# Differential attention: the probability tiles transposed by DMA from SBUF halves instead of by TensorE

## The chip, the cores and the metric

The kernel runs on one core of one Trainium2 chip. The metric is the device time of one execution in microseconds (us). Times of the kernel before are the median of three runs; one further execution was recorded by the hardware profiler, and all rows below come from it.

## The reference, cut to what matters

The program is a two-layer block of a diffusion transformer on 512 latent and 256 context tokens of width 1024. Layer 1 ends in a mixture of experts. Before that it has two kinds of attention side by side: a windowed attention, and the differential attention that this change concerns:

```python
def diff_attend(q, kvs, lam):
    ss = [einsum('bhiqd,bhikd->bhiqk', q, k) * scale for k, _ in kvs]
    ps = joint_softmax(ss)                       # over latent and context keys together
    for p, (_, v) in zip(ps, kvs):
        a = p[:, :, 0] - lam * p[:, :, 1]        # two softmaxes, subtracted
        out = out + einsum('bhqk,bhkd->bhqd', a, v)
```

There are 4 heads, each with two softmaxes over 768 keys, and 512 queries. Everything is float32 to the outside; the kernel splits each operand of a matmul into two float16 halves, `hi` and `lo = x - hi`.

## The kernel before, in words

The program is written for a framework that takes the instructions in the order of the Python code, gives each tile a buffer out of a pool, and then orders each engine's queue itself. Each engine runs its queue in order.

`diff` (line 1393) handles 4 blocks of 128 queries with 8 units each: unit m is one softmax of one head, so two units, a pair, make one head. 16 pairs follow each other, counted here from 0 to 15. For a pair:

- `scores` (L1422): eight matmuls (L770) write both units' scores `dS`, 128 x 768 float32 each, into PSUM. There are two such buffers, so the next pair's first matmul waits for this pair's exponentials.
- `probs` (L1432): VectorE takes the row maximum (L1435, `dnm`), ScalarE the exponential (L1438, `dP`) with the row's sum. The even unit's tile is `P0`. For the odd unit VectorE makes a factor out of both sums (L1443, L1444, `dden`), and GpSimd multiplies P by it (L1446) and adds P0 (L1447). P0's pool has 4 buffers.
- `transp` (L1450): calls `p_transp` (L1351). TensorE transposes P in six 128 x 128 float32 chunks into two PSUM tiles `PT` of three chunks (L1360); for each of them ScalarE writes `Phi`, the float16 half (L1361), and VectorE subtracts to get `Plo` (L1362), both out of PSUM. Phi and Plo have 2 buffers each.
- `pv` (L1457): twelve matmuls (L1467, L1468) multiply the six chunks of Phi and Plo with the values into `dO`.

`attention` (L772) emits, at step i, scores of unit i, transp of unit i - DLAG[1], and pv of unit i - DLAG[2]. After the last head of a query block a chain of small VectorE operations (L1481 to L1490, `rs_of` at L315, with names dr, dss, rs_v, rs_r, rs_t, don) normalizes it, and L1383 to L1390 put it into `yT`.

`layer1` (L1516) runs the first units beside the last projection (`psdv`, the values, L347 to L349, with L637 and L638 after each token tile), then the rest of the pairs, and then interleaves the end of `diff` with the first half of the output projection `od_out(0)` (tile `odps`, L342) by the weights DIFF_W and OUT_W. Beside it GpSimd gathers the residual `h` from DRAM (L1560) and SyncE loads weights (`wst`, L246) that ScalarE and VectorE split into halves (`whi` L269, `wlo` L274). SyncE's queue is in order as well: a load waits there until its buffer's last split is done.

Of the kernel before, what the change touches and what calls it, by code (L numbers as in the profile page):

```python
# [12 lines left out]
F16 = mybir.dt.float16  # L13
BF = mybir.dt.bfloat16
I32 = mybir.dt.int32
AF = mybir.ActivationFunctionType
OP = mybir.AluOpType
# [25 lines left out]
PB2 = 6  # L43
NLAG = (0, 3, 4)
SLAG = (0, 2, 3)
DLAG = (0, 6, 8)

GEMM_W, SWA_W, DIFF_W, OUT_W = 42.0, 50.0, 40.0, 24.0
NDIF = 4

NSTEP1 = (0, 2, 3, 3)
# [254 lines left out]
class K:  # L306
# [1086 lines left out]
    def diff(self, T, yT, ap, p2, pp, tpb):  # L1393
        nc = self.nc
        Qd, Kd, Vd = T['dq'], T['dk'], T['dv']
        units = [dict(q=n, m=m) for n in range(4) for m in range(8)]
        den, O, osum, P0 = {}, {}, {}, {}
        pend = []

        def flush(d=3):  # L1400
            for p in pend:
                p[0] += 1
            while pend and pend[0][0] > d:
                z = pend.pop(0)
                z[1]()
                self.ndiff = z[2] + 1

        def products(u):
            n, m = u['q'], u['m']
            if m == 0:  # L1410
                den[n] = ap.tile([128, 8], F32, name=f"dden{n}", tag="den", bufs=2)
            u['S'] = ps = pp.tile([128, 1024], F32, name=f"dS{n}_{m}", tag="S", bufs=2)
            qs = slice(n * 128, n * 128 + 128)
            b = 64 * (m % 2)
            full, half = [], []
            for bank, (k0, kn) in enumerate(CHUNKS):
                o = ps[:, k0:k0 + kn]
                full.append((o, Qd[:, m, qs], Kd[:, m, k0:k0 + kn], bank))
                half.append((o, Qd[b:b + 64, m, qs], Kd[b:b + 64, 8 + m // 2, k0:k0 + kn], bank))
            return full, half  # L1420

        def scores(u):  # L1422
            if u['m'] % 2:
                return 0.0
            i = 8 * u['q'] + u['m']
            pair = units[i:i + 2]
            self.paired(*[products(z) for z in pair])
            for z in pair:
                probs(z)
            return 1.2  # L1430

        def probs(u):  # L1432
            n, m, ps = u['q'], u['m'], u.pop('S')
            nm = ap.tile([128, 1], F32, name="dnm", tag="dnm", bufs=4)
            nc.vector.tensor_reduce(out=nm, in_=ps[:, 0:NT], axis=AX.X, op=OP.max, negate=True)  # L1435
            P = (p2 if m % 2 else ap).tile([128, 768], F32, name="dP", tag="P", bufs=PB2 if m % 2 else PB)
            dn = den[n][:, m:m + 1]
            nc.scalar.activation(P, ps[:, 0:NT], AF.Exp, bias=nm, accum_out=dn)  # L1438
            if m % 2 == 0:
                P0[n] = P  # L1440
            else:

                nc.vector.reciprocal(dn, dn)  # L1443
                nc.vector.scalar_tensor_tensor(out=dn, in0=dn, scalar=self.nlam, in1=den[n][:, m - 1:m], op0=OP.mult,  # L1444
                                               op1=OP.mult)
                nc.gpsimd.tensor_scalar(P, P, dn, 1.0, op0=OP.mult, op1=OP.mult)  # L1446
                nc.gpsimd.tensor_tensor(out=P, in0=P, in1=P0[n], op=OP.add)  # L1447
                u['P'] = P

        def transp(u):  # L1450
            if u['m'] % 2 == 0:
                return 0.0
            flush()
            u['PT'] = self.p_transp(u.pop('P'), 6, ap, pp, tpb)
            return 0.65

        def pv(u):  # L1457
            n, m = u['q'], u['m']
            if m % 2 == 0:
                return 0.0  # L1460
            hd = m // 2
            hi, lo = u.pop('PT')
            if hd % 2 == 0:
                O[n] = pp.tile([128, 2, 2, 128], F32, name=f"dO{n}_{hd}", tag="G", bufs=2)
            o = O[n][:, hd % 2]
            for i in range(6):
                nc.tensor.matmul(o, hi[:, i, :], Vd[:, i, hd], start=i == 0, stop=False)  # L1467
                nc.tensor.matmul(o[:, 0, :], lo[:, i, :], Vd[:, i, hd, 0], start=False, stop=i == 5)  # L1468
            if hd == 0:
                osum[n] = ap.tile([128, 4, 128], F32, name=f"osum{n}", tag="osum", bufs=1)  # L1470
            if hd % 2 == 1:
                nc.vector.tensor_reduce(out=osum[n][:, hd - 1:hd + 1], in_=O[n].rearrange("p h s d -> p h d s"),
                                        axis=AX.X, op=OP.add)
            if hd == 3:
                os_ = osum[n]
                sq = ap.tile([128, 4, 128], F32, name="dsq", tag="dsq", bufs=1)
                ss = ap.tile([128, 4], F32, name="dss", tag="dss", bufs=2)
                for i in range(4):
                    nc.scalar.activation(sq[:, i], os_[:, i], AF.Square, accum_out=ss[:, i:i + 1])
                r0 = ap.tile([128, 4], F32, name="dr0", tag="dr0", bufs=2)  # L1480
                nc.vector.reciprocal(r0, den[n][:, 0:8:2])  # L1481
                r2 = ap.tile([128, 4], F32, name="dr2", tag="dr2", bufs=2)
                nc.vector.tensor_tensor(out=r2, in0=r0, in1=r0, op=OP.mult)
                nc.vector.tensor_tensor(out=ss, in0=ss, in1=r2, op=OP.mult)
                rs = self.rs_of(ap, ss, 4, 128, "sub")
                nc.vector.tensor_tensor(out=rs, in0=rs, in1=r0, op=OP.mult)
                for i in range(4):
                    nc.scalar.activation(os_[:, i], os_[:, i], AF.Copy, scale=rs[:, i:i + 1])
                on = ap.tile([128, 512], F32, name="don", tag="dsq", bufs=1)
                nc.vector.tensor_tensor(out=on.rearrange("p (h d) -> p h d", h=4), in0=os_,  # L1490
                                        in1=self.gsub.unsqueeze(1).broadcast_to([128, 4, 128]), op=OP.mult)
                self.o_out(on, 512, yT, 4, n, ap, pp, pend, tpb)
                pend[-1].append(n)
            return 1.0

        yield from self.attention(units, [scores, transp, pv], DLAG)
        flush(0)

# [570 lines left out]
```

## Time and profile before

| what | us |
|---|---|
| median of 3 runs | 1780.31 |
| lowest and highest of them | 1778.89, 1789.47 |
| profiled execution, its own time | 1788.69 |
| its span, first to last instruction | 1786.8 |
| mean granted TensorE clock in it | 0.977 of full |

The page of the profile has the busy time of each engine, then the span in 40 slices of 44.7 us, in which a digit is the busy tenths of that slice. The differential attention lies at 1113.9 to 1224.5 us, in the slices 25 to 28 (the first slice is 1). Idle time in a row is that just before the instruction, with what released it.

### The profile page before, as it was taken

To read this page: it belongs to the slowest core of one execution; us is meant where nothing else is said; L and a number is where in the kernel's file an instruction comes from. 1 tells how busy PE (TensorE), PEld (TensorE's weight loads), DVE (VectorE), ACT (ScalarE), POOL (GpSimd) and SP (SyncE) were. 2 spreads that over 40 slices of the span, in tenths; PEclk is the share of its full clock that TensorE was granted. 3 is DMA by queue.
4 is the path that set the end of the run, shared out by engine and by line. 5 is a ranking of instruction groups with operands and counts; after the bars stand their busy time and mean duration, and the time that the engine had idled before them with its cause. 6 is when DMAs were issued, how large, how long until landed. Compare 5 with 4: busy or idle time off the path is not lost. (4 is left out here: it accounts for less than half of the span.)

```text
span 1786.8 us, 36195 instructions
## 1 busy us (share of the span) xinstructions
PE 1668.7 (93%) x15124; PEld 1170.3 (65%) x15124; DVE 1251.0 (70%) x2463; ACT 883.1 (49%) x1420; POOL 156.1 (9%) x102
## 2 busy tenths in 40 slices
PE   3999999999999999999999999989789999999997
PEld 1444666555566665555555466447579988989997
DVE  6784899877665444333147999696898588788884
ACT  6564555262222222111254667564666577677773
POOL 1100000000000000000000000451210113101201
PEclk9999999999999999999999999999799999999999
DMA  8413342534333442233312201101569788899893
GB/s 322 160 51 100 104 166 95 212 117 143 142 129 131 142 142 96 73 112 112 115 61 79 95 1 48 70 3 54 189 204 337 240 312 334 303 330 336 313 337 109
DMA packets 51801, 286.82 MB, mean 161 GB/s; under 512 B 5824, under 2 KB 10944, under 8 KB 27568
## 3 DMA queue, kind: packets, MB, share of 16 engines
q1 hardware_dynamic: 47328, 271.74, 41.8%
q0 software_dynamic: 3296, 10.95, 2.7%
q8 instruction: 120, 1.97, 0.4%
q10 hardware_dynamic: 1008, 1.77, 0.3%
q14 instruction: 49, 0.40, 0.1%
HBM read 272.57 MB, written 11.08 MB: 159 GB/s over the span
## 5 line engine op out<-in xcount | busy, mean ns | idle before, releaser
L342 PEld LDWEIGHTS <-whi 128*128 128x128 f16 x5184 | 469.7, 99 | 185.3 <-issue 10.8
L342 PE MATMUL f<-yT,whi 128*128 128x512 f16 (+1 forms) x1408 | 325.5, 326 | 1.5 <-ACT af L438 1.5
L342 PEld LDWEIGHTS <-wlo 128*128 128x128 f16 x2592 | 255.6, 99 | 90.4 <-issue 2.2
L274 DVE SCALAR_TENSOR_TENSOR wlo<-wst,whi 128x512 f16<-128x512 f32 (+2 forms) x154 | 236.8, 1549 | 68.1 <-ACT whi L269 67.6
L269 ACT ACTIVATE whi<-wst 128x2048 f16<-128x2048 f32 (+2 forms) x152 | 199.4, 1331 | 111.1 <-PE f L342 72.8
L342 PE MATMUL f<-yT,wlo 128*128 128x512 f16 (+1 forms) x704 | 229.1, 326 | 0.0
L375 DVE SCALAR_TENSOR_TENSOR adjk<-wst,srow 128x1024 bf16<-128x1024 f32 x96 | 117.3, 1221 | 98.4 <-DMA wst<-in_w_adr_dram 97.2
L342 PE MATMUL f<-gT,whi 128*128 128x512 f16 (+1 forms) x704 | 164.4, 326 | 0.0
L342 PE MATMUL mps<-xT,whi 128*128 128x176 f16 (+6 forms) x1472 | 149.0, 229 | 3.8 <-DVE mgf L1848 3.7
L342 PE MATMUL mps<-xT,wlo 128*128 128x176 f16 (+6 forms) x736 | 143.0, 229 | 0.0
L342 PE MATMUL f<-gT,wlo 128*128 128x512 f16 (+1 forms) x352 | 114.7, 326 | 0.0
L342 PEld LDWEIGHTS <-aT 128*128 128x128 f16 x1584 | 106.8, 99 | 5.3 <-issue 4.5
L467 DVE TENSOR_TENSOR h<-h,ytp 128x256 f32<-128x256 f32 (+1 forms) x48 | 24.3, 507 | 109.2 <-PE ytp L465 108.9
L2019 POOL DMA_INDIRECT out_dram<-yr,sidx x14 | 54.4, 3885 | 358.3 <-DVE yr L1884 215.3
L342 PE MATMUL cvps<-aT,whi 128*128 128x512 f16 (+1 forms) x384 | 82.6, 328 | 2.8 <-ACT Kl L632 2.3
L342 PEld LDWEIGHTS <-whix 128*128 128x128 f16 x992 | 81.4, 98 | 2.9 <-issue 2.5
L1082 ACT CAST gT<-g 128x512 f16<-128x512 f32 (+1 forms) x23 | 14.0, 608 | 131.0 <-DVE g L1079 131.0
L274 DVE SCALAR_TENSOR_TENSOR wlo<-wstx,whi 128x2048 f16<-128x2048 f32 (+2 forms) x42 | 68.7, 1651 | 14.0 <-ACT whi L269 11.4
L342 PE MATMUL mps<-xT,aT 128*128 128x176 f16 (+6 forms) x1056 | 74.4, 231 | 2.3 <-DVE mgf L1848 2.3
L342 PE MATMUL mps<-mgT,whi 128*128 128x176 f16 (+6 forms) x704 | 73.0, 227 | 0.9 <-ACT mgT L1853 0.9
L342 PE MATMUL mps<-mgT,wlo 128*128 128x176 f16 (+6 forms) x352 | 68.1, 227 | 0.0
L269 ACT ACTIVATE whi<-wstx 128x2048 f16<-128x2048 f32 (+2 forms) x42 | 57.7, 1401 | 17.6 <-PE mps L342 16.3
(398 smaller groups left out, 3490.1 us busy)
## 6 DMA issues: line engine op xcount, KB each, us to landing
wst<-in_w_m_dram SPq DMA_DIRECT2D x38, 1024.0 KB, 6.2
wstx<-in_w_m_dram SPq DMA_DIRECT2D x33, 1024.0 KB, 6.2
wst<-in_w_adr_dram SPq DMA_DIRECT2D x32, 1024.0 KB, 4.9
wst<-in_w_f_dram SPq DMA_DIRECT2D x22, 1024.0 KB, 4.8
wst<-in_w_m_dram SPq DMA_DIRECT2D x27, 704.0 KB, 6.0
wstx<-in_w_m_dram SPq DMA_DIRECT2D x25, 704.0 KB, 6.1
aT<-in_w_m_dram SPq DMA_DIRECT2D x17, 1024.0 KB, 6.2
wst<-in_w_ada_dram SPq DMA_DIRECT2D x12, 1024.0 KB, 4.9
```

Of the source, the lines that this page charges most:

```text
L269: nc.scalar.activation(h, x, AF.Copy, scale=self.scale)
L274: nc.vector.scalar_tensor_tensor(out=l, in0=x, scalar=SW, in1=h, op0=OP.mult, op1=OP.subtract)
L342: mm(ps[:, s0:s0 + sn], w[:, k, :], a[:, kk, s0:s0 + sn], start=first and p == 0, stop=last and p == 2)
L375: nc.vector.scalar_tensor_tensor(out=jk, in0=st[:, j * D:(j + 1) * D], scalar=1.0, in1=self.srow[:, t, :], op0=OP.mult, op1=OP.mult, accum ...
L467: nc.vector.tensor_tensor(out=hs, in0=hs, in1=tp[:, 0:w].rearrange("p (t c) -> p t c", t=nt), op=OP.add)
L1082: nc.any.tensor_copy(gh, g[:, 0:sn])
L2019: self.nc.gpsimd.indirect_dma_start(out=to, out_offset=bass.IndirectOffsetOnAxis(ap=self.sidx[0:sn, e, s:s + 1], axis=0), in_=yr[0:sn, s, ...
```

## The change

`transp` no longer calls `p_transp`. ScalarE copies the finished P, in SBUF, to float16 in one instruction over all 768 columns (after: L1457), VectorE subtracts that from P in one instruction over SBUF operands (after: L1458), and both halves go into the 3072 bytes a row of the pair's P0 tile, which is free once GpSimd has added it. SyncE then issues two transposing DMAs, SBUF to SBUF, 128 x 768 float16 each (192 KB), into Phi and Plo (after: L1462). P0's buffer is free again only when both have landed. The distance DLAG[1] goes from 6 units to 4, and DIFF_W from 40 to 30, as transp's own weight goes from 0.65 to 0. `swa` still uses `p_transp`.

```diff
-DLAG = (0, 6, 8)
-GEMM_W, SWA_W, DIFF_W, OUT_W = 42.0, 50.0, 40.0, 24.0
+DLAG = (0, 4, 8)
+GEMM_W, SWA_W, DIFF_W, OUT_W = 42.0, 50.0, 30.0, 24.0
...
-                u['P'] = P
+                u['P'], u['P0'] = P, P0[n]
...
             flush()
-            u['PT'] = self.p_transp(u.pop('P'), 6, ap, pp, tpb)
-            return 0.65
+            P = u.pop('P')
+            z = u.pop('P0').bitcast(F16).rearrange("p (z c) -> p z c", z=2)
+            nc.scalar.activation(z[:, 0], P, AF.Copy)
+            nc.vector.tensor_tensor(out=z[:, 1], in0=P, in1=z[:, 0], op=OP.subtract)
+            u['PT'] = []
+            for i, nm in enumerate(("Phi", "Plo")):
+                t = ap.tile([128, 6, 128], F16, name=nm, tag=nm, bufs=2)
+                nc.sync.dma_start_transpose(out=t, in_=z[:, i])
+                u['PT'].append(t)
+            return 0.0
```

VectorE's queue in the third query block, at the row maxima of the pair with units 4 and 5 and the small chain of the first block; before:

```order
L1435 TENSOR_REDUCE dnm<-dS_4_12248 128x1
L331 TENSOR_TENSOR rs_t<-rs_r 128x4
L1444 SCALAR_TENSOR_TENSOR dden_12148<-dden_12148,nlam 128x1
L332 SCALAR_TENSOR_TENSOR rs_t<-rs_t,rs_v 128x4
L1435 TENSOR_REDUCE dnm<-dS_5_12249 128x1
L333 SCALAR_TENSOR_TENSOR rs_r<-rs_t,rs_r 128x4
L1362 TENSOR_TENSOR Plo<-PT,Phi 128x384
L1486 TENSOR_TENSOR rs_r<-rs_r,dr_12119 128x4
L1362 TENSOR_TENSOR Plo<-PT,Phi 128x384
L1435 TENSOR_REDUCE dnm<-dS_6_12297 128x1
```

The same place in the changed kernel:

```order
L1435 TENSOR_REDUCE dnm<-dS_4_12198 128x1
L331 TENSOR_TENSOR rs_t<-rs_r 128x4
L1444 SCALAR_TENSOR_TENSOR dden_12114<-dden_12114,nlam 128x1
L332 SCALAR_TENSOR_TENSOR rs_t<-rs_t,rs_v 128x4
L1435 TENSOR_REDUCE dnm<-dS_5_12199 128x1
L333 SCALAR_TENSOR_TENSOR rs_r<-rs_t,rs_r 128x4
L1458 TENSOR_TENSOR dP<-dP 128x768
L1495 TENSOR_TENSOR rs_r<-rs_r,dr_12085 128x4
L1435 TENSOR_REDUCE dnm<-dS_6_12239 128x1
```

The two subtractions from PSUM have become one from SBUF; what stands around it is as before. Four of the sixteen new subtractions stand further ahead, among the last row maxima beside the values' projection, and the one below is the fourth of them, with the split of an output weight behind it:

```order
L1458 TENSOR_TENSOR dP<-dP 128x768
L638 SCALAR_TENSOR_TENSOR dqv<-psdv_11820,dqv 128x4x128
L638 SCALAR_TENSOR_TENSOR dqv<-psdv_11847,dqv 128x4x128
L274 SCALAR_TENSOR_TENSOR wlo_12557<-wst_11636,whi_12556 128x2048
L638 SCALAR_TENSOR_TENSOR dqv<-psdv_11874,dqv 128x4x128
L1435 TENSOR_REDUCE dnm<-dS_0_11914 128x1
```

Before, all 32 subtractions stood behind the last L638. ScalarE's queue in the second query block, with what each instruction waits for (DMAHW is a DMA's landing); in the changed kernel:

```order
L1438 ACTIVATE dP,dden_11913<-dS_2_11956,dnm 128x768 [waits DMAHW6_49,DMAHW5_49,DVE_49]
L1438 ACTIVATE dP,dden_11913<-dS_3_11957,dnm 128x768 [waits DVE_49]
L1457 ACTIVATE dP<-dP 128x768 [waits Activation_49,Pool_49]
L1438 ACTIVATE dP,dden_11913<-dS_4_11997,dnm 128x768 [waits DMAHW1_49,DMAHW0_49,DVE_49]
L1438 ACTIVATE dP,dden_11913<-dS_5_11998,dnm 128x768 [waits DVE_49]
L1457 ACTIVATE dP<-dP 128x768 [waits Activation_49,Pool_49]
```

Each even unit's exponential now waits for the two transposes of four pairs earlier, whose source lies in its buffer, and the copy of a pair stands right behind the exponentials of the next. SyncE's queue in the changed kernel has the transposes around the first two loads of expert weights:

```order
L1462 DMA_TRANSPOSE Phi<-dP 128x6x128
L1462 DMA_TRANSPOSE Plo<-dP 128x6x128
L246 DMA wst_12560<-in_w_m_dram 128x2048
L1462 DMA_TRANSPOSE Phi<-dP 128x6x128
L1462 DMA_TRANSPOSE Plo<-dP 128x6x128
L1462 DMA_TRANSPOSE Phi<-dP 128x6x128
L1462 DMA_TRANSPOSE Plo<-dP 128x6x128
L246 DMA wst_12566<-in_w_m_dram 128x2048
```

Before, those two loads stood next to each other; four transposes stand ahead of the first, four between them, and twenty-four behind the second.

## Rows read from the trace of the kernel before

**Rows 1.** The page: busy time and share of each engine (the first line of its part 1), then TensorE's busy tenths and the granted clock in 40 slices.

```profile
PE 1668.7 (93%) x15124; PEld 1170.3 (65%) x15124; DVE 1251.0 (70%) x2463; ACT 883.1 (49%) x1420; POOL 156.1 (9%) x102
...
PE   3999999999999999999999999989789999999997
...
PEclk9999999999999999999999999999799999999999
```

**Rows 2.** Windows of the stage: from and to, length, then busy time (and instructions) of PE, PEld, DVE, ACT and POOL, the granted clock, DMA share, GB/s.

```profile
1122.00:1152.00 30.00, 29.99 (x149) 12.85 (x149) 16.36 (x26) 13.73 (x26) 12.01 (x9) 1.00 0.00 1
1152.00:1160.00 8.00, 6.22 (x49) 3.91 (x47) 7.35 (x14) 6.23 (x11) 4.79 (x5) 1.00 0.82 316
1160.00:1206.00 46.00, 38.60 (x263) 22.57 (x262) 44.78 (x94) 32.48 (x85) 27.05 (x20) 0.93 0.04 14
1206.00:1225.00 19.00, 16.60 (x161) 13.87 (x160) 16.76 (x42) 9.49 (x30) 7.98 (x4) 1.00 0.18 58
```

**Rows 3.** Groups by line in 1106 to 1226 us: line, engine, operation, count, then busy us and mean ns, then idle before.

```profile
L1447 POOL TENSOR_TENSOR dP<-dP 128x768 f32<-128x768 f32 x16 | 32.0, 2001 | 1.3
L1435 DVE TENSOR_REDUCE dnm<-dS 128x1 f32<-128x768 f32 x32 | 30.2, 947 | 3.4 <-PE dS L770 3.1
L770 PE MATMUL dS<-Kd,dqv 128*128 128x512 f16 (+3 forms) x128 | 29.6, 329 | 4.8 <-ACT dP L1438 4.8
L1438 ACT ACTIVATE dP<-dS,dnm 128x768 f32<-128x768 f32 x32 | 28.7, 900 | 6.4 <-DVE dnm L1435 5.2 <-DVE rs_t L331 0.8
...
L1360 PE MATMUL PT<-ident,dP 128*128 128x128 f32 x96 | 18.1, 300 | 4.8 <-DVE Plo L1362 3.8 <-DVE h L467 0.9
```

**Rows 4.** The tiles Phi and Plo in 1150 to 1225 us: count, duration in ns as least/median/most, first and last start.

```profile
L1361 ACT ACTIVATE Phi<-PT x32: 472/491/498, 1151.1 to 1220.4; 128x384 f16<-128x384 f32 x32
...
L1468 PE MATMUL dO<-dqv,Plo x96: 219/219/314, 1153.8 to 1224.5; 128*128 128x128 f16 x96
L1362 DVE TENSOR_TENSOR Plo<-PT,Phi x32: 520/545/558, 1152.7 to 1221.2; 128x384 f16<-128x384 f32 x32
```

**Rows 5.** Groups by form over the whole program, on VectorE and on ScalarE: the two operations of 128 x 768 from float32 in SBUF to float16 in SBUF (they belong to layer 0).

```profile
L984 DVE TENSOR_TENSOR yT<-yc,yT 128x768 f16<-128x768 f32 x4 | 3.8, 948 | 0.0
...
L983 ACT ACTIVATE yT<-yc 128x768 f16<-128x768 f32 x4 | 3.4, 845 | 9.6 <-DVE yc L981 9.6
```

**Rows 6.** Time lines of VectorE, then of GpSimd: start, length, instruction.

```profile
1171.51 1.52 DVE L322 TENSOR_SCALAR rs_r<-rs_v 128x4 int32<-128x4 int32 x1
...
1175.73 0.55 DVE L1362 TENSOR_TENSOR Plo<-PT,Phi 128x384 f16<-128x384 f32 x1
1176.19 1.52 DVE L332 SCALAR_TENSOR_TENSOR rs_t<-rs_t,rs_v 128x4 f32<-128x4 f32 x1
...
1210.98 2.25 DVE L274 SCALAR_TENSOR_TENSOR wlo<-wst,whi 128x2048 f16<-128x2048 f32 x1
...
1213.63 1.29 DVE L1483 TENSOR_TENSOR dr<-dr 128x4 f32<-128x4 f32 x1
...
1216.32 0.15 DVE L332 SCALAR_TENSOR_TENSOR rs_t<-rs_t,rs_v 128x4 f32<-128x4 f32 x1
...
1175.88 1.81 POOL L1447 TENSOR_TENSOR dP<-dP 128x768 f32<-128x768 f32 x1
...
1211.08 3.83 POOL L1447 TENSOR_TENSOR dP<-dP 128x768 f32<-128x768 f32 x1
```

**Rows 7.** Time lines: the first exponential of pair 4 on ScalarE, then on VectorE the row maximum of the last pair of the second block and of the last pair of the third.

```profile
1154.88 0.90 ACT L1438 ACTIVATE dP<-dS,dnm 128x768 f32<-128x768 f32 x1
...
1182.79 0.94 DVE L1435 TENSOR_REDUCE dnm<-dS 128x1 f32<-128x768 f32 x1
...
1203.77 0.94 DVE L1435 TENSOR_REDUCE dnm<-dS 128x1 f32<-128x768 f32 x1
```

**Rows 8.** The DMA view of the whole program (a queue: packets, MB, share of 16 engines' span; then issues with their count, KB of each, and median us from issue to landing), and one window of 4 us.

```profile
q10 hardware_dynamic: 1008, 1.77, 0.3%
...
wst<-in_w_odo_dram SPq DMA_DIRECT2D x4, 1024.0 KB, 5.1
...
V<-V SPq DMA_DIRECT2D x6, 128.0 KB, 2.3
...
cstm<-in_consts_dram ACTq DMA_DIRECT2D x1, 210.5 KB, 2.5
...
wr<-in_w_rt_dram ACTq DMA_DIRECT2D x1, 32.0 KB, 1.6
...
1154.00:1158.00 4.00, 3.36 (x27) 1.90 (x25) 3.44 (x6) 2.74 (x6) 2.44 (x3) 1.00 1.00 397
```

**Rows 9.** Windows of 2 us in the third block, columns as in rows 2.

```profile
1182.00:1184.00 2.00, 1.25 (x9) 0.54 (x8) 2.00 (x5) 1.45 (x5) 0.38 (x1) 1.00 0.01 4
1184.00:1186.00 2.00, 1.13 (x6) 0.30 (x5) 2.00 (x6) 2.00 (x5) 0.42 (x1) 1.00 0.00 0
1186.00:1188.00 2.00, 2.00 (x14) 1.61 (x13) 2.00 (x4) 0.38 (x2) 1.92 (x2) 0.58 0.00 0
```

**Rows 10.** Who waited for whom in 1106 to 1226 us (us in total, times, longest), and GpSimd's first addition.

```profile
PE dS L770 <- ACT dP L1438: 4.8, 8, 1.4
...
1128.46 1.80 POOL L1447 TENSOR_TENSOR dP<-dP 128x768 f32<-128x768 f32 x1
```

## The prediction

> **What bounds the kernel now.** I read the page first. TensorE is busy for 93% of the program, and the slices show where it is not: the digits 8, 9, 7, 8 in the slices 25 to 28 are the differential attention, and one of them has a lower granted clock [rows 1]. The mean says nothing about that stage, so the second view is the windows [rows 2], and they give three parts. Until 1152 TensorE is full (29.99 of 30 us), since the values' projection runs beside the first pairs, and VectorE is busy for only 16.36. From 1160 to 1206 it is the other way round: VectorE 44.78 of 46, TensorE 38.60, ScalarE 32.48. After 1206 the output projection is mixed in. So in the middle VectorE sets the pace. The third view is two time lines: between the last row maxima of the second and the third query block lie 20.98 us for four pairs [rows 7], 5.2 us for a pair. The waits agree: TensorE waited only 4.8 us for exponentials in the whole stage [rows 10]. A change is worth here what it does to VectorE between 1152 and 1222, unless its new transfers become slower than 5.2 us for a pair.
>
> **VectorE's own work.** The 32 subtractions from PSUM go, 0.545 us each [rows 4]: -17.4 us, all behind the last L638 and so all in the part that VectorE bounds. The 16 new ones have the form of L984, 128 x 768 from float32 in SBUF to float16 in SBUF: 0.948 us [rows 5]. Four of them stand, by the changed order, ahead of the last L638, in the part where VectorE idles 13.6 of 30 us and TensorE is the bound [rows 2]; that idle time hides 4 x 0.948 = 3.8 us. If it did not, 3.8 is the price. The other twelve cost 12 x 0.948 = +11.4. Term 1: -17.4 + 11.4 = -6.0 us.
>
> **ScalarE and TensorE.** ScalarE loses 32 x 0.491 = 15.7 us [rows 4] and gets 16 x 0.845 = 13.5 [rows 5]; it has 13.5 us free of 46 where VectorE is full, so I count nothing. TensorE loses 96 transposes of 300 ns by mean, 18.1 us with their overlaps [rows 3]. It was idle 7.4 of 46 us in that part already, so this is worth nothing by itself. The lags are free too: the copy of a pair now stands behind the next pair's exponentials but one, and GpSimd's multiply and add (27.05 of 46 us busy) are done by then.
>
> **VectorE against GpSimd.** The time lines show something that the sums hide [rows 6]. At 1176.19 a VectorE operation on 128 x 4 numbers took 1.52 us; the same line took 0.15 at 1216.32. In the first case GpSimd's addition L1447 ran from 1175.88 for 1.81 us, and VectorE's operation ended with it. Eight of the twelve additions from 1159 to 1215 have such a stalled small operation beside them, the first at 1171.51 (1.52 us) and the last at 1213.63 (1.29). The subtraction L1362 at 1175.73, which reads PSUM, ran beside the start of the same addition in its usual 0.55. It can go the other way: at 1211.08 an addition took 3.83 us beside a split L274 of 2.25 us, both operands of which lie in SBUF. In this trace, then, VectorE and GpSimd get in each other's way where VectorE works on SBUF alone. The new subtraction does; the old one did not. Bounds: no new stall (0), if the new subtractions meet the additions that were stalling something anyway, or if GpSimd waits instead, which has time; or the four additions that were free so far each cost some 1.4 us (1.52 less 0.15): +5.5. A gain is left out, since the small chains stay. I take +5.5, because eight of twelve met one already with few SBUF operations about. Term 2: +5.5 us.
>
> **The transposes.** No row of the trace shows a transposing DMA. Two per pair, 192 KB each, go from SyncE's queue. How much they may take follows from the buffers. Phi and Plo have two each, so the transposes of pair k+2 start when the products of pair k are done, and the products of pair k+2 and the exponential of pair k+6 come two pairs later, 10.4 us. Two landings of 5 us behind each other fit in this; as throughput, 5.2 / 2 = 2.6 us for a half. From below, the nearest rows are plain transfers [rows 8]: SBUF to SBUF, 128 KB in 2.3 us (V<-V), and 210.5 KB in 2.5 us from issue to landing. That is about 2.5 us for 192 KB, overlapping in the queue: hidden, 0 us. From above, the rows of a transpose could go as small packets: 768 pieces of 256 bytes in a half. The queue q10 moved 1008 packets in 0.3% of 16 x 1786.8 us, 85 ns for a packet [rows 8]; 768 x 85 ns / 16 engines = 4.1 us for a half, more than 2.6. I take the row of V<-V, the same way from SBUF to SBUF and near in size, and add 1 us, because at 1154 to 1158 the DMA engines are full (share 1.00, 397 GB/s) with the gathers of h and a weight load [rows 8], just when the first pairs' transposes land. On SyncE's queue eight transposes stand ahead of the first two loads and 24 behind the second; each of the loads has a 1 MB landing of 5.1 us [rows 8] and the first use of the weights comes with the output projection, after 1206. Term 3: +1 us, with 0 to +48 and more as its bounds (the rivals).
>
> The Trainium skill speaks for it: "DMA: Bandwidth & Descriptors", section "Latency and other measured facts", gives a transposing DMA an effective 261 GB/s. By that my estimate for 192 KB is 0.75 us beside the latency, and the term would be 0. No run here shows it so far.
>
> **The sum.** -6.0 + 5.5 + 1 = +0.5 us. It is worked out on the profiled execution, 1788.69 us, which is 8.4 above the median of the runs shown, 1780.31; I carry only the difference over: about 1781. Its own range is 1770 (no new stall, and TensorE's waits of 4.8 us gone) to 1800 (the four hidden subtractions in the open, and transposes that are late by 1 us for each of the 14 later pairs).
>
> **Rivals.**
>
> *The queue of transposes becomes the bound* (slower). The place is SyncE's queue from pair 2 on; the price is 4.1 us for a half, 8.2 for a pair, from the packet row above; it decides from 2.6 us for a half. The pairs 0 and 1 land beside the values' projection, since GpSimd's first addition is at 1128.46 [rows 10]. From pair 4's first exponential at 1154.88 [rows 7] the 14 others would take 14 x 8.2 = 115 us, to about 1271, and the last product 2 later, against 1224.5 now [rows 4]: +48, about 1828. For it: small packets are what transposing 2-byte elements could come to. Against it: V<-V is SBUF to SBUF too, and costs its 2.3 us.
>
> *Each 128 x 128 chunk is a transfer of its own, one after the other* (slower still). A 32 KB transfer took 1.6 us (wr) [rows 8]; six are 9.6 us for a half, 19.2 for a pair, 269 for 14 pairs: about +200, near 1980. Against it: that row is mostly latency, which transfers in one queue share.
>
> The Trainium skill has a rule that speaks against this change: "VectorE: DVE Perf Modes", section "The three transpose paths", has 1309 ns for a 128 x 128 block of bfloat16 by DMA against 390 ns by TensorE. If six blocks of it stood behind each other, a half would be 7.85 us, 14 pairs 220 us, and the time by my estimate about 1934. Nothing in this trace shows which of the two pages holds for a transpose of six blocks.
>
> *VectorE's gain stays whole.* No new stall against GpSimd, and TensorE's 4.8 us of waits go too: -6.0 - 4.8 = -10.8, about 1770. It lies within 1%. For it: GpSimd has time to wait itself. Against it: eight of twelve.
>
> *TensorE's clock falls.* With 18 us less work TensorE idles more. After two windows of 1.25 and 1.13 busy of 2 us the granted clock was 0.58 in the next [rows 9], near the lower level of 1.2 GHz. The scores take 29.6 / 16 = 1.85 us for a pair [rows 3]; 12 pairs at the lower level would be up to +22, about 1803. Against it: much of it would fall into TensorE's idle time, and in that part the mean clock was still 0.93 [rows 2].
>
> **Chances.** The forecast 0.57; the queue as bound 0.23; single chunks 0.08; the whole gain 0.07; the clock 0.05. 1% of this kernel, 17.8 us, is about what a measurement of it can tell from no change. The second and third rivals, and most of the clock's, are slower by more: 0.33 with the tail of the forecast below 0.01. Faster by more needs term 1 with all sixteen subtractions hidden: 0.06, taken from the forecast and the whole gain. The rest, 0.61, is within 1%. The range goes from 1771, the whole gain, to 1835, above the queue rival; the single chunks and both tails stay out.
>
> **What would show it.** Right: the new subtractions at about 0.95 us, some at up to 2.4 beside a GpSimd addition; transposes that land in 2 to 5 us; VectorE still over 95% busy in the middle and 5 us a pair; the last product near 1225. Wrong: landings over 5 us, SyncE's queue never empty from 1156 on, exponentials that wait for a landing, the last product near 1270 or later. The clock's rival would show as a granted clock near 0.5 over several windows, with the scores of a pair near 3.7 us. If the subtractions ran in under 0.6 us, or all sixteen beside the projection, term 1 would be too small.

## The result and the profile after

| what | before | after |
|---|---|---|
| median, us (6 runs each) | 1783.92 | 1802.05 |
| lowest and highest, us | 1778.89, 1789.47 | 1800.02, 1805.69 |
| ratio of the times, 95% interval | 1 | 1.0095 [1.0080, 1.0110] |
| span of the profiled execution, us | 1786.8 | 1799.0 |

The change costs 0.95% of the time, some 17 us. That is within 1%, where the likeliest case stood, but at the edge of it, since the interval reaches to 1.10%. The forecast was 1781, and the measured time lies in its range. The two profiled executions differ by 12.2 us: that of before took 1788.69 us, 4.8 over the median of its runs, and that of after 1800.77, 1.3 under. Between them the stage accounts for all of the difference; where the other 5 us of the 17 lie is not shown.

The page after: busy time of each engine, then TensorE's busy tenths and clock in 40 slices of 45.0 us (the differential attention is again in the slices 25 to 28).

```profile
PE 1662.6 (92%) x15028; PEld 1158.1 (64%) x15028; DVE 1250.3 (70%) x2447; ACT 882.6 (49%) x1404; POOL 152.0 (8%) x102
...
PE   3999999999999999999989999778788998999997
...
PEclk8999999999999999999999999879889999999999
```

Against [rows 1], TensorE's tenths in these four slices are 9, 7, 7, 8 where they were 9, 9, 8, 9, and the clock in the slices 26 and 27 reads 8 and 7 where it was full. The windows, columns as in [rows 2], say more:

```profile
1122.00:1152.00 30.00, 29.04 (x142) 12.12 (x140) 17.52 (x28) 16.34 (x27) 12.68 (x9) 1.00 0.14 27
1152.00:1160.00 8.00, 3.58 (x28) 1.85 (x26) 7.18 (x10) 5.12 (x12) 6.59 (x6) 0.86 0.85 244
1160.00:1206.00 46.00, 29.44 (x160) 13.78 (x160) 32.80 (x58) 22.05 (x52) 24.21 (x15) 0.72 0.61 122
...
1158.00:1166.00 8.00, 0.00 (x0) 0.00 (x0) 1.19 (x3) 2.83 (x5) 2.79 (x3) 0.50 1.09 221
```

From 1160 to 1206 VectorE is busy for 32.80 us, where it was 44.78: it no longer sets the pace there. The last row shows where most of that went: from 1158 to 1166 TensorE does nothing at all and VectorE 1.19 us, while the DMA engines are full. Who waits there is in the time lines (first SyncE's queue, then TensorE, then VectorE; a bracket is the idle time before an instruction and what ended it):

```profile
1136.07 1.24 SPq L1462 DMA_TRANSPOSE Plo<-dP  x1
1152.17 0.36 SPq L246 DMA_DIRECT2D wst<-in_w_m_dram  x1
1153.09 1.53 SPq L1462 DMA_TRANSPOSE Phi<-dP  x1
1154.72 4.03 SPq L1462 DMA_TRANSPOSE Plo<-dP  x1
1158.85 3.04 SPq L1462 DMA_TRANSPOSE Phi<-dP  x1
1161.98 4.90 SPq L1462 DMA_TRANSPOSE Plo<-dP  x1
1166.93 0.57 SPq L246 DMA_DIRECT2D wst<-in_w_m_dram  x1
...
1166.96 0.40 PE L1476 MATMUL dO<-dqv,Phi 128*128 128x256 f16 x1 [10.48 <-DMA Phi<-dP]
...
1158.24 0.95 DVE L1435 TENSOR_REDUCE dnm<-dS 128x1 f32<-128x768 f32 x1
1171.14 0.96 DVE L1435 TENSOR_REDUCE dnm<-dS 128x1 f32<-128x768 f32 x1 [11.96 <-PE dS L770]
```

The transposes of pair 2 are issued at 1153.09 and 1154.72, right behind a 1 MB weight load and beside the four gathers of h, which GpSimd issues from 1150.76 to 1156.01. TensorE's next products wait for Phi until 1166.96, and since its queue is in order the next scores stand behind them; VectorE idles for 11.96 us and no row maximum begins between 1158.24 and 1171.14. The landings (least, median and most, us) of the transposes into Phi and into Plo:

```profile
DMA to landing us min/median/max: 2.7/2.8/13.8
...
DMA to landing us min/median/max: 2.7/2.8/12.8
```

The DMA view of the whole program, with the median from issue to landing, for both and for the gathers:

```profile
Phi<-dP SPq DMA_TRANSPOSE x16, 2.8
Plo<-dP SPq DMA_TRANSPOSE x16, 2.8
...
h<-h_spill,nat POOLq DMA_INDIRECT x4, 9.4
```

A transpose of 192 KB lands in 2.8 us as a rule, and in up to 13.8 us beside the gathers. Who waited for whom from 1106 to 1240 us, which answers to [rows 10]:

```profile
ACT dP L1457 <- POOL dP L1447: 22.3, 15, 3.5
DVE dnm L1435 <- PE dS L770: 16.1, 7, 12.0
PE dO L1476 <- DMA Phi<-dP: 13.7, 3, 10.5
PE dS L770 <- ACT dP L1438: 6.7, 7, 2.2
```

The groups of the new operations from 1100 to 1260 us, which answer to [rows 4, 5]:

```profile
L1458 DVE TENSOR_TENSOR dP<-dP 128x768 f16<-128x768 f32 x16 | 17.3, 1081 | 6.6 <-ACT dP L1457 6.6
...
L1457 ACT ACTIVATE dP<-dP 128x768 f16<-128x768 f32 x16 | 13.5, 842 | 22.3 <-POOL dP L1447 22.3
```

And the last products, from the tile dO (as in [rows 4], least/median/most in ns, then first and last start):

```profile
L1477 PE MATMUL dO<-dqv,Plo x96: 217/219/314, 1151.6 to 1236.5; 128*128 128x128 f16 x96
```

The last product comes at 1236.5 against 1224.5. After that the kernels take the same: 562.3 us to the end of the span before, 562.5 after.

To compare stages of runs that begin a few us apart, four times of each profile are used below: the first row maximum, the second row maximum of pair 6, that of pair 15, and the last product. Their differences, in us, read from the time lines (e3 is not among them: its profiled execution was a slow one, 1956 us against its median of 1806):

| kernel | to pair 6 | pair 6 to 15 | to the last product | sum |
|---|---|---|---|---|
| before | 39.7 | 42.2 | 19.8 | 101.7 |
| after | 51.6 | 46.3 | 17.1 | 115.0 |
| e1, gathers spread | 43.2 | 53.7 | 17.2 | 114.0 |
| e2, before, gathers spread | 39.8 | 43.0 | 21.1 | 103.9 |
| e4, before, numbers alone | 42.8 | 42.6 | 19.9 | 105.3 |
| f1, no gathers | 42.9 | 47.2 | 17.3 | 107.4 |
| f2, idle transposes | 48.6 | 46.1 | 19.7 | 114.4 |
| f3, plain transfers | 47.7 | 45.3 | 16.1 | 109.1 |
| f4, four buffers | 41.7 | 49.1 | 14.7 | 105.5 |
| g1, f4 and later copy | 43.7 | 48.9 | 13.8 | 106.4 |
| g2, f4 and filler | 46.1 | 45.6 | 14.4 | 106.1 |
| h1, f4 and late filler | 42.0 | 45.9 | 14.4 | 102.4 |
| h2, before, late filler | 40.9 | 46.9 | 18.2 | 106.0 |

Between before and after the sum grows by 13.3 us, of which 11.9 up to pair 6, where the long wait lies. The second and third column belong together, since the products stand closer to the scores in the changed kernels: 62.0 us before, 63.4 after.

### The profile page after: what moved, and what is told of

It is laid out like the page before. It is cut to its first block, busy times and chain, and to the rows that moved or that the text cites. A ratio compares the mean times of both kernels' runs of the same rounds, so it can differ in the third digit from the quotient of the medians.

```text
span 1799.0 us, 36047 instructions
## 1 busy us (share of the span) xinstructions
PE 1662.6 (92%) x15028; PEld 1158.1 (64%) x15028; DVE 1250.3 (70%) x2447; ACT 882.6 (49%) x1404; POOL 152.0 (8%) x102
## 3 DMA queue, kind: packets, MB, share of 16 engines
q1 hardware_dynamic: 72928, 278.03, 44.0%
## 5 line engine op out<-in xcount | busy, mean ns | idle before, releaser
L2028 POOL DMA_INDIRECT out_dram<-yr,sidx x14 | 47.1, 3367 | 357.6 <-DVE yr L1893 213.6
```

Source lines behind the costliest of these rows:

```text
L2028: self.nc.gpsimd.indirect_dma_start(out=to, out_offset=bass.IndirectOffsetOnAxis(ap=self.sidx[0:sn, e, s:s + 1], axis=0), in_=yr[0:sn, s, ...
```

## The experiments

Theory 1: the loss is the late landing beside the gathers. Theory 2: ScalarE's in-order queue is held up by the copy, which waits for GpSimd's addition. The rivals: TensorE's lower clock; the changed numbers DLAG and DIFF_W by themselves; the transposing form of the transfer.

**e1, the gathers spread** over the pairs 5, 7, 9 and 11.

```diff
-                for t in range(4):
-                    nc.gpsimd.indirect_dma_start(out=self.h[:, t, :], ...)
+                def gather(t, d):
+                    nc.vector.tensor_copy(self.h[:, t, 0:1], d)
+                    nc.gpsimd.indirect_dma_start(out=self.h[:, t, :], ...)
...
+                k = 4 * n + m // 2
+                if k in GATH:
+                    self.hgather(GATH.index(k), dn)
...
+        GATH = (5, 7, 9, 11)
```

> The changed kernel, with the four gathers of h (512 KB each) no longer together at 1150 to 1156 us but each behind a tiny VectorE write that waits for pair 5, 7, 9 or 11. Theory 1 (the transposes of pairs 2 and 3 land late, 13.8 to 7.0 us, because they share the DMA engines with 2 MB of gathers and a 1 MB load): their landings fall below 6 us, TensorE's wait of 10.5 us for Phi is under 3, and the last product comes 8 to 11 us earlier, near 1227; time about 1792. Rival (transposes are slow behind the 1 MB load in SyncE's queue, whatever GpSimd gathers): landings stay at 9 us or more, the wait stays over 8 us, time within 3 us of the changed kernel's.

Measured: 1801.12 us against 1785.13, ratio 1.0070 [1.0046, 1.0093]. The landings of Phi and TensorE's waits:

```profile
DMA to landing us min/median/max: 2.7/4.2/5.7
```

```profile
PE dO L1482 <- DMA Plo<-dP: 7.9, 4, 3.8
PE dO L1481 <- DMA Phi<-dP: 7.6, 4, 2.9
```

Phi's landings fell under 6 us, Plo's to 7.9 at most, and the wait of 10.5 is gone, so that it is the gathers that delay transposes was right; the rest of the expectation was wrong. The waits are now many and short, 15.5 us in sum, and the pairs 6 to 15 take 53.7 us. Four of the five longest waits, 1.9 to 3.8 us, end 5 to 9 us after one of the four gathers was issued: each gather delays the transposes that it meets, and spreading them only spreads the loss.

**e2, the same in the kernel before.**

> The kernel before, with the same four gathers spread in the same way: the control of the first run. Both theories: no wait in the stage depends on the gathers there, so the time is that of before within 5 us and the last product stays within 2 us of 1224.7. If it becomes faster by more, the gain of the first run is not the transposes' own.

Measured: 1788.78 us, ratio 1.0009 [0.9995, 1.0023], last product at 1226.1. As expected: without transposing DMAs nobody waits for the place of the gathers.

**e3, the copy on GpSimd.**

```diff
-            nc.scalar.activation(z[:, 0], P, AF.Copy)
+            nc.gpsimd.tensor_copy(z[:, 0], P)
```

> The changed kernel, with the float16 copy on GpSimd instead of ScalarE. Theory 2 (from pair 6 on the pace, 46.3 us for nine pairs against 42.2 before, is set by ScalarE, whose queue waits 22.3 us in sum for GpSimd's addition ahead of the copy and holds up the next exponential): ScalarE's waits for GpSimd go, and nine pairs take 42 us or less unless GpSimd, which gets 16 copies of about 0.9 us or more, becomes the bound at over 4.6 us a pair. Rival (the lower granted clock sets the pace, 0.50 in much of 1182 to 1216): no change in the pace, 46 us within 1. Either way the wait near 1158 to 1167 stays; time 1796 by the theory, 1802 by the rival.

Measured: 1806.19 us, ratio 1.0107 [1.0090, 1.0124]. No gain. The expectation had an exception, a GpSimd that becomes the bound itself; no profile of e3 can be compared with the others, so that stays open, and e3 decides nothing about theory 2.

**e4, the numbers alone:** DLAG (0, 4, 8) and DIFF_W 30 in the kernel before.

> The kernel before with the changed DLAG (0, 4, 8) and DIFF_W 30 alone, TensorE still transposing. Theories 1 and 2: the numbers alone do nothing, time within 6 us of before. Rival (the order of the work, not the transposes, made the difference): at least 10 us slower than before.

Measured: 1791.93 us, ratio 1.0033 [1.0019, 1.0047]: slower by 5.9 us, at the edge of what was expected. In the kernel before, the numbers cost 3.1 us up to pair 6, as pair 3's maxima fall behind the values' projection (at 1152.8 and 1153.7, where they stood at 1132.6 and 1134.0). In the changed kernel they stay ahead of its end (1131.7 and 1135.7), so this loss is not in it. What else the numbers do there was not tried.

**f1, no gathers.** GpSimd writes a constant into h; the residual is left out, so the experts behind get other loads, and only the stage is read, not the time of the whole (3390 us).

```diff
-                    nc.gpsimd.indirect_dma_start(out=self.h[:, t, :], ...)
+                    nc.gpsimd.memset(self.h[:, t, :], 0.5)
```

> The changed kernel without the four gathers: GpSimd writes a constant into h in their place, so the 2 MB are not moved (the residual is left out). Theory 1 (the landings of transposes beside the gathers are what was lost): all transposes land in 2.7 to 4 us, TensorE's long wait for Phi goes, the pace from pair 6 to 15 is at or under the 42.2 us of before, and the last product comes at 1224 or earlier; time 1780 to 1786. Rival (landings are long because of the 1 MB load that SyncE issues just ahead, or of the transposes' own queue): a landing over 8 us stays, time over 1795. Second rival (TensorE's lower clock sets the pace): the long wait goes, but nine pairs still take 46 us or more, time 1790.

Measured: to pair 6 42.9 us, where after had 51.6, the sum 107.4. TensorE's waits for Phi in the stage:

```profile
PE dO L1476 <- DMA Phi<-dP: 3.4, 3, 2.1
```

The long wait is gone with the gathers, although the 1 MB load is still there: theory 1 holds against the load as the cause. (The trace of f1 has no landing times of the transposes, so only the waits are read.) Two parts of theory 1's expectation missed: the pairs 6 to 15 still take 47.2 us, and the sum is 5.7 over that of before. Both are what the second rival, the clock, had said; the granted clock from 1160 to 1206 was 0.73. The next run asks for it.

**f2, the transposes of TensorE as idle work.**

```diff
+            for c0 in (0, 3):
+                tp = pp.tile([128, 4, 128], F32, name="PT", tag="PT", bufs=tpb)
+                for c in range(3):
+                    nc.tensor.transpose(tp[:, c, :], P[:, (c0 + c) * 128:(c0 + c + 1) * 128], self.ident)
```

> The changed kernel plus the 96 TensorE transposes of before, into PSUM tiles that nobody reads. The clock rival (with 18 us less work TensorE idles, its granted clock falls to 0.50 and the scores of a pair take up to 3.7 us in place of 1.85): the mean granted clock from 1172 to 1222 rises from 0.76 to 0.9 or more, pace of nine pairs falls from 46 to 43, time 1797 or less. Theory 1: TensorE gets 18 us more work, the late landings stay as they are; time the same as the changed kernel's or up to 8 us more.

Measured: 1805.68 us, ratio 1.0112 [1.0082, 1.0143]. The window from 1172 to 1222:

```profile
1172.00:1222.00 50.00, 39.50 (x260) 22.81 (x258) 43.95 (x87) 30.00 (x69) 30.46 (x20) 0.90 0.44 80
```

The clock rose from 0.76 to 0.90, and the pairs 6 to 15 took 46.1 us, where the changed kernel took 46.3. So raising the clock in this way wins nothing. It doesn't clear the clock altogether, since f2 also gives TensorE 18 us more work, which can hide a gain.

**f3, plain transfers** in place of the transposing ones (the transposition is left out, so again only the stage is read).

```diff
-                nc.sync.dma_start_transpose(out=t, in_=z[:, i])
+                nc.sync.dma_start(out=t, in_=z[:, i].rearrange("p (c k) -> p c k", c=6))
```

> The changed kernel with plain SBUF to SBUF transfers of the same halves (the transposition is left out). Theory 1 in its narrow form (any small transfer that shares the DMA engines with the gathers is late): the transfers of pairs 2 and 3 still land in 8 us or more, time within 4 us of the changed kernel's. Rival (the transposing form itself is the matter: 1.2 us to issue each, small elements, packets that crawl beside others): landings under 5 us beside the gathers, 2 to 2.5 us elsewhere, the long wait is gone, time 1792 or less.

Measured: 3383 us for the whole, which is not compared; the sum of the stage is 109.1 us. The landings of the transfers that write Phi, and TensorE's wait for them:

```profile
DMA to landing us min/median/max: 2.1/5.9/9.7
```

```profile
PE dO L1476 <- DMA Phi<-dP: 5.1, 3, 4.1
```

A plain transfer of the same halves lands in 9.7 us too in the worst case. So a plain transfer suffers beside the gathers as well, and the transposing form makes it longer (13.8, and 10.5 us as the longest wait in place of 4.1). Neither side of the expectation was quite right.

**f4, four buffers for Phi and Plo.**

```diff
-PB2 = 6
+PB2 = 5
...
-                t = ap.tile([128, 6, 128], F16, name=nm, tag=nm, bufs=2)
+                j = u['m'] // 2 % 2
+                t = (p2 if j else ap).tile([128, 6, 128], F16, name=nm, tag="d" + nm if j else nm, bufs=2)
```

> The changed kernel with four buffers for Phi and Plo in place of two (PB2 is 5 for their room). In the changed kernel pair 2's transposes are issued at 1153, after the products of pair 0 at 1151.5 have freed the buffers, though its sum was done by 1143. Theory 1: with four buffers the transposes of pairs 2 and 3 are issued before 1150, ahead of load and gathers, land in 3 us, the wait of 10.5 us is gone, the last product comes 8 to 12 us earlier, time 1790 to 1795. Rival (the transfers of the stage are slow as such, and the next pairs' take over the wait): TensorE's waits for Phi and Plo stay over 10 us in sum, time within 3 us of the changed kernel's.

Measured: 1791.69 us, ratio 1.0026 [1.0012, 1.0040]. SyncE's queue:

```profile
1139.21 1.21 SPq L1463 DMA_TRANSPOSE Phi<-dP  x1
1140.46 1.29 SPq L1463 DMA_TRANSPOSE Plo<-dP  x1
1144.38 1.21 SPq L1463 DMA_TRANSPOSE Phi<-dP  x1
1145.69 1.23 SPq L1463 DMA_TRANSPOSE Plo<-dP  x1
1153.05 5.46 SPq L246 DMA_DIRECT2D wst<-in_w_m_dram  x2
```

The waits in the stage:

```profile
PE dS L770 <- ACT dP L1438: 12.4, 9, 3.2
DVE dnm L1435 <- PE dS L770: 7.8, 11, 1.4
PE dO L1477 <- DMA Phi<-dP: 1.6, 2, 1.0
```

The transposes of the pairs 2 and 3 now leave at 1139 to 1146, ahead of load and gathers, and the wait for Phi is 1.6 us in sum. With the same gathers and the same transposes the time falls from 1.0095 to 1.0026 of before: 0.69%, some 12 us of the 17, as theory 1 expected. f4 takes the meeting with gathers and load away, f1 the gathers alone, and in both the long wait goes: together they show theory 1.

What is left, 0.26%, may lie in the two other rows. VectorE waits 7.8 us for scores, where it waited 3.1 [rows 3], and TensorE 12.4 us for exponentials, where it waited 4.8 [rows 10]. There VectorE's saving became waiting. (The profile is of the longest of f4's ten executions, 1796.80 us, so its rows may overstate what is left.) The next three changes ask for its cause.

**g1, f4 and the copy later**, so that it is no longer ahead of exponentials that are ready.

```diff
-            nc.scalar.activation(z[:, 0], P, AF.Copy)
+            j = 8 * u['q'] + u['m'] + 3
...
+            nc.scalar.activation(one, units[j]['dn'], AF.Copy, scale=0.0, bias=1.0)
+            nc.scalar.activation(z[:, 0], P, AF.Copy, scale=one)
```

> Four buffers as in f4_four_buffers, and ScalarE's copy of a pair tied to the first exponential of the next pair but one (its scale is a 1 made out of that exponential's sum on ScalarE, 14 times some 0.25 us), so that in ScalarE's queue the copy no longer waits for GpSimd ahead of exponentials that are ready. Theory 2 for what is left (in f4_four_buffers ScalarE waits 21.7 us in sum for GpSimd ahead of copies, TensorE 12.4 us for exponentials): these waits fall under 8 us and 6 us, VectorE's idle time in the pairs 6 to 15 falls from 6.8 us to under 3, the last product comes 2 to 5 us earlier after the first maximum (105.5 us in f4, 101.7 in the kernel before), time within 3 us of before or under it. Rival (VectorE's sum of work, stalls included, sets the pace whatever ScalarE does): 105.5 us within 1.5, time as f4.

Measured: 1792.07 us, ratio 1.0035 [1.0021, 1.0050]. The waits in the stage:

```profile
PE dO L1483 <- DMA Phi<-dP: 8.3, 3, 7.2
PE dO L1484 <- DMA Plo<-dP: 7.7, 7, 1.9
PE dS L770 <- ACT dP L1438: 4.1, 5, 1.2
ACT dP L1463 <- POOL dP L1447: 3.8, 2, 3.0
```

ScalarE's wait for GpSimd fell to 3.8 us (from 21.7) and TensorE's for exponentials to 4.1, as theory 2 wanted; but the transposes leave later now, and TensorE waits 16.0 us for them. The longest wait, 7.2 us, is for pair 2's Phi: it is issued at 1155.96 now, beside the gathers again, and lands in 6.9 us. So g1 brings a part of theory 1's loss back while it takes theory 2's waits away, and cannot tell what those waits cost. Theory 2 is neither borne out by a time in any run nor refuted.

**g2, f4 and filler for TensorE's clock.**

```diff
+            tp = pp.tile([128, 4, 128], F32, name="PF", tag="PT", bufs=tpb)
+            for c in range(8):
+                nc.tensor.transpose(tp[:, c % 4, :], self.ident, self.ident)
```

> Four buffers as in f4_four_buffers, and eight TensorE transposes of a constant for each pair (no operand to wait for, results unread, 2.4 us a pair) to keep TensorE busy. The clock rival for what is left (granted clock 0.72 from 1172 to 1222 where before had 0.93, so that the scores of a pair take up to 3.7 us): the clock rises over 0.9, VectorE's waits for scores (7.8 us) fall under 4, and the last product comes 2 us or more earlier after the first maximum than f4's 105.5 us; time 1786 to 1790. Theory 2 (ScalarE's queue): clock up, but 105.5 us or more, time as f4 or up to 5 us more.

Measured: 1791.97 us, ratio 1.0029 [1.0012, 1.0047]. The window from 1172 to 1222:

```profile
1172.00:1222.00 50.00, 39.25 (x287) 25.27 (x287) 49.38 (x88) 30.85 (x76) 28.99 (x19) 0.93 0.47 77
```

The clock is at 0.93 again, where f4 had 0.72, and VectorE is busy for 49.38 of 50 us; from pair 6 on the stage takes 60.0 us against f4's 63.8. VectorE's waits for scores fell to 2.9 us, as the clock rival expected, but neither the sum (106.1 us) nor the time did. What the filler brings was lost ahead, where it lengthens the values' projection (its last matmul begins at 1154.3, in f4 at 1151.0; 46.1 us to pair 6).

**h1, f4 and the filler from pair 4 on** (`if u['q']:` ahead of g2's lines).

> Four buffers as in f4_four_buffers, and the filler of g2_clock_filler (eight TensorE transposes of a constant for each pair, unread) from pair 4 on alone, so that it no longer lengthens the values' projection. In g2 the first maximum of pair 4 came 3.4 us later than in f4, and from the last maximum of pair 6 to the last product were 60.0 us against 63.8 in f4 and 62.0 before. If two causes, the landings and the clock, hold all of the loss: first maximum to pair 6 as f4 (41.7 us), the rest as g2 (60), the last product 101.7 us after the first maximum, as before (101.7); time within 4 us of before. If the remainder of f4 is something else (GpSimd, ScalarE's queue): 104 us or more, and 4 us or more over before.

Measured: 1793.52 us, ratio 1.0045 [1.0031, 1.0060].

**h2, the same filler in the kernel before.**

> The kernel before with the same filler from pair 4 on: the control. TensorE's clock is at 0.93 there already (1160 to 1206) and TensorE has its transposes, so 2.4 us more a pair costs a little or nothing: the last product 101 to 107 us after the first maximum, time between 2 us less and 8 us more than before. If it gains more than 2 us, the filler's gain in the changed kernel is not due to the change.

Measured: 1788.77 us, ratio 1.0031 [1.0016, 1.0046].

h2 came out as expected, in the time and in the stage (106.0 us). In its one profile h1's stage came out as expected as well, 102.4 us, but its 12 times, from 1786.2 to 1798.8, are no better than f4's: 8 us over before, where two causes alone were to give 4 at most. The profile (1788.54 us) is at the low end of these times, f4's at the high end of its own, and the times decide. By them the filler costs 0.31% in the kernel before and about 0.2% (1.0045 less 1.0026) on f4; a difference of 0.1% is inside the intervals. So a share of the clock in the rest is not shown, and something else is in it. No version tried is faster than the kernel before.

## Why the prediction was right or wrong

**The likeliest case**, within 1%, came true, but not by its sum. The sum gave +0.5 us, and some 17 were measured. That this stayed within 1% is luck: the interval of the ratio reaches over it. What held: ScalarE and TensorE had room, and a transpose lands in 2.8 us as a rule, close to the 2.5 that was taken from the rows of plain transfers [rows 8] and under the 5 us that two buffers allow. What did not: VectorE was to stay over 95% busy in the middle, and was busy for 32.80 of 46 us; the last product was to come near 1225, and came at 1236.5; and a landing over 5 us, named as a sign of being wrong, came with 13.8.

**The queue rival** is refuted as a rate: two halves issued some 1.3 us apart land 2.8 us after their issue each, so they overlap, and SyncE's queue is idle between pairs. Its picture of the packets was right: 25600 packets came in (72928 less 47328 in SyncE's queue), 800 for a half, where 768 had been counted. Their price was not: the queue's share rose from 41.8% to 44.0% of 16 engines' span, by my estimate some 715 us of one engine, 28 ns a packet in place of 85. Single chunks one after the other are refuted by the same 2.8 us. From the Trainium skill's "VectorE: DVE Perf Modes", section "The three transpose paths", my estimate was 7.85 us for six blocks in a row; the trace does not agree with that estimate.

**A slip in the reading** changed no term: the digits 8, 9, 7, 8 of [rows 1] stand in the slices 27 to 30, not 25 to 28, so that only the first two of them belong to the stage, and the lower clock stands in slice 29, behind it. The sums rest on the windows.

**The step that failed is the 1 us of term 3.** I had the place: the first pairs' transposes land when the gathers and the load fill the DMA engines (share 1.00). I priced it at 1 us, as if a full engine delayed a transfer by its own length. It is 10.5 us of TensorE's time [the row at 1166.96], because a landing took 13.8 us; f4 takes the meeting away and gets back some 12 us. Two things that stood in the profile of before were left out. The gathers are 2 MB, and the load 1 MB: at 397 GB/s [rows 8] that is, as an estimate, some 8 us of full engines, and a transfer that starts in the middle of it and shares them may end no sooner than they do. For the plain transfers of f3 that is about the size (9.7 us at most). For transposes it is still too little: with them under way the engines moved only 221 GB/s from 1158 to 1166, and in f1, beside the weight loads alone, 214 GB/s at a DMA share of 1.19 (1154 to 1158). And the two buffers of Phi and Plo hold pair 2's transposes back until the products of pair 0 are done, so that they are issued at 1153 though their sum was ready by 1137.4 and the second half by 1139.3. I used the two buffers for the rate alone and not for the first start.

**Term 1.** Four of the sixteen new subtractions did lie in VectorE's idle time (1129.80, 1134.77, 1138.33 and 1143.51), and an undisturbed one took 0.94 to 0.99 us, as taken from L984. The saving of 6.0 us did not become time, though: in f4, where the late landing is out of the way, 0.26% is still lost, and in its profile VectorE waits for scores 4.7 us more than before.

**Term 2** was too large in its place. The sixteen subtractions took 17.3 us, 2.1 more than 16 x 0.948, and that is two of them, the last but two and the last but one, both beside an addition of GpSimd (1220.66 and 1225.55):

```profile
1221.03 2.56 DVE L1458 TENSOR_TENSOR dP<-dP 128x768 f16<-128x768 f32 x1
1224.91 1.36 DVE L1458 TENSOR_TENSOR dP<-dP 128x768 f16<-128x768 f32 x1
```

The stall of 1.4 us beside GpSimd's additions stayed with the small operations, which it had hit before [rows 6], as this pair of the changed kernel shows:

```profile
1182.78 1.76 DVE L332 SCALAR_TENSOR_TENSOR rs_t<-rs_t,rs_v 128x4 f32<-128x4 f32 x1
...
1182.06 2.46 POOL L1447 TENSOR_TENSOR dP<-dP 128x768 f32<-128x768 f32 x1
```

**"GpSimd's multiply and add are done by then"** was wrong. The copy of a pair stands right behind the exponentials of the next pair, and ScalarE waits 22.3 us there in 15 places. Where that wait is removed (g1), another takes its place, so no time shows what it costs. Nor was "the lags are free too" right for the kernel before, where the new numbers alone cost 0.33% (e4).

**The clock's rival** has its picture and not its price. The granted clock was 0.72 from 1160 to 1206 and 0.50, the lower level of 1.2 GHz, from 1158 to 1166, where TensorE did nothing. Raised to 0.90 by 18 us of idle transposes (f2), it brought nothing.

What stays open is the remainder, 0.26% in f4. The filler that raises the clock does not give it back (g2, h1), and the run that takes ScalarE's waits away brings a late landing back (g1). A rival that was not tried is the numbers: alone, in the kernel before, they cost 0.33% (e4), as much as what is left, and no run has the transposing DMAs with the old ones. The path from GpSimd's sum to the products is also longer by a copy, a subtraction, 1.2 us of issue and 2.8 us of landing, and that alone may be what VectorE's 4.7 us of waits are; this is argued and not shown.

## What to carry to other kernels

Work that is moved from an engine to the DMA engines gets a new neighbour: look for the largest transfer that is under way when the moved work's first results are due, and take its whole remaining time as the price, not the moved transfer's own; here even that was too little for the transposing form. A buffer count that allows the rate in the steady part can still hold the first transfers back until they meet that neighbour; two more buffers were worth some 12 us here. And what the move frees is worth only as much as the engine that sets the end gets: 18 us of TensorE bought nothing.

## What the runs showed of the hardware that was not expected

- A transposing DMA of 192 KB holds SyncE's queue for 1.21 us where a plain one of that size holds it for 0.47 (f3), and up to 4.90 us while other transfers fill the engines:

```profile
1161.44 0.47 SPq L1462 DMA_DIRECT2D Phi<-dP  x1
```

- Four gathers of 512 KB on GpSimd's queue delay a small transfer on SyncE's queue far beyond its own length: up to 13.8 us for a transposing and 9.7 us for a plain one, against 2.7 and 2.1 alone. A 1 MB load is under way with them; with the load and no gathers TensorE's longest wait for Phi was 2.1 us (f1). The gathers suffer too, 9.4 us by median in place of 6.2 before and in f4.
- The DMA share goes over 1 with transposes under way (1.09 from 1158 to 1166, and 1.11 in the row below, which has the second weight load) while the bytes fall to 221 and 286 GB/s, from 397 with the same gathers and no transposes [rows 8]. It is the transposes that go with the fall: without gathers it is 214 GB/s (f1, 1154 to 1158), and with plain transfers beside the gathers 420 (f3, 1158 to 1162, share 1.06):

```profile
1166.00:1172.00 6.00, 4.78 (x23) 2.40 (x23) 0.86 (x1) 0.00 (x0) 0.00 (x0) 0.55 1.11 286
```
